# A hybrid attention and delta-rule block: frozen engine orders and four value blocks as seven half products

## The chip, the cores and the metric

The kernel runs on one core of a Trainium2 chip. The metric is the device time of one execution in microseconds, as a median of several. TensorE is called PE in the profile, VectorE DVE, ScalarE ACT, GpSimd POOL and SyncE SP.

## The reference

One residual layer on x of 1024 tokens by 1024 channels in float32. After an RMS norm, one input projection of 8208 columns feeds two mixers and their gates:

```python
h = _rmsnorm(x, norm_w[layer])
proj = h @ w_in[layer]
dsa_qkv, dsa_z, gdn_qkv, gdn_z, gdn_b, gdn_a, gate_a, gate_b = _split_columns(proj)
# mixer A: three groups of 8 heads x 64, windows and dilations (128,1), (512,4), (2048,16)
q_a = _apply_rope(qkv[:, :, :, 0], cos, sin)
k_a = _apply_rope(qkv[:, :, :, 1], cos, sin)
v_a = qkv[:, :, :, 2]
o_a = _dilated_mixture(q_a, k_a, v_a).astype(x.dtype)
y_a = (o_a * jax.nn.silu(dsa_z)) @ w_up_a[layer]
# mixer B: gated delta rule, 8 heads x 64, in chunks of 64 tokens, after a short causal conv
o_b = _gated_delta_rule(gq, gk, gv, g, beta)
y_b = (o_b * jax.nn.silu(gdn_z)) @ w_up_b[layer]
merged = jax.nn.sigmoid(gate_a) * y_a + jax.nn.sigmoid(gate_b) * y_b
x = x + merged @ w_out[layer]
```

A final RMS norm follows. The values v_a of the three groups are what the first half of the change touches: each is a plain product of h with 512 columns of w_in.

## The kernel before

**Numbers.** Each float32 operand of a projection is split into two float16 parts, hi and lo. A product is then three float16 matmuls per k tile (hi x hi, hi x lo, lo x hi), issued by `mm3_steps` (L183 to L185). The split is two instructions: ScalarE writes hi (`w_hi`, L166, or L330), VectorE writes lo with a `scalar_tensor_tensor` (the helper at L83, as a plain `tensor_tensor` is at L86).

**Units.** The input projection is cut in units of 256 output columns: 18 for attention (`att_unit(g, hs, what)`: group, half of the heads, and query, key or value), 6 for the delta rule, 4 of SiLU gates and 8 of sigmoid gates. A unit's weights come by two DMAs of 512 KB on GpSimd's queue into `wstage` (two buffers), and are split into `whi` and `wlo` (two buffers each). There are two kinds of unit. `Normal` multiplies all of h by the unit. `Seven` cuts h and the unit in halves both ways and forms seven products of half size in place of eight, from sums of the blocks of h (made once, `sums_of_h`) and of the weights (made per unit on VectorE, L329). `seven_products` runs them in three PSUM banks, with three ScalarE copies (L367) of a product that enters two outputs. The list `SEVENS` says which units are `Seven`: before, the queries and keys of groups 1 and 0, three sigmoid gates and all four SiLU gates.

Queries, keys and gates have channels on the output partitions, so the stationary operand is the weight block and 512 tokens stream past it (`proj`, `by_channel`). Values have tokens on the partitions: the stationary operand is 128 tokens of h, and the unit's 256 columns stream past it (`v_unit`, `gen`; matmuls `ps_mm<-whi,h_hi` of 128x256). Group 1 takes its 128 tokens at a stride of four (`tok`), group 2 at eight, group 0 packed.

**Order of TensorE.** TensorE's instructions are in the order of the program text, which interleaves two things by hand: `Feed` gives out the units in steps of some 0.65 us, and the attention (`att_run`), the delta rule's pieces and its scan take steps between them at set paces. `Feed.ahead` places the load and the splits of the next unit at set steps of the present one. In the attention's step, scores go to PSUM, VectorE masks them and takes the minimum (L799, tile `sm`), ScalarE takes the exponential (L803), TensorE transposes (L813), ScalarE and VectorE split the result into `th` and `tl` (L818, L86), and TensorE multiplies by the values (L836 to L840).

**Order of the others.** VectorE, ScalarE and the DMA queues are ordered by the framework's own scheduler, with hints: `tc.high_priority` around what evicts PSUM, `SOLVE_LATER` for the triangular solve, and `in_turn`, which ties some instructions to a place behind the matmul issued last in the text:

```python
def in_turn(i):
    if last_pe[0]:
        tc.add_manual_dep(i.ins, last_pe[0], order_only, reason="in turn")
```

Two stretches are fixed by hand on VectorE and ScalarE as well, with `manual_schedule`: the start (until the first query and key products are done) and the end of the last pair of token tiles.

**Stages, in us of the profile:** start to 62, attention beside the input units to 560, delta rule's preparation beside its units (convolutions `ca`, decay, solve, merge, `state_parts` with the copies `uw`) to 785, scan over 16 chunks beside the SiLU and gate units to 912, up projections to 995, output projection to the end.

Of the kernel before, what the change touches and what calls it, by code (L numbers as in the profile page):

```python
# [2 lines left out]

# [30 lines left out]
def att_unit(g, hs, what):  # L34
    return U_ATT + (g * 2 + hs) * 3 + what


def gdn_unit(hb, what):
# [39 lines left out]
def hybrid_block(ctx: ExitStack, tc: tile.TileContext, A):  # L78
# [7 lines left out]
        (eng or V).tensor_tensor(out, in0, in1, op)  # L86

    ctx.enter_context(tc.manual_schedule(engines={nc.tensor.engine}))
    base = ctx.enter_context(tc.tile_pool(name="base", bufs=1))
    ps = ctx.enter_context(tc.tile_pool(name="ps", bufs=1, space=PSUM))  # L90

# [57 lines left out]
    first = base.tile([128, 1], F32, name="first")  # L149
    SC.activation(first, epsc, AF.Sqrt)  # L150

    last_pe = [None]
    order_only = mybir.DependencyInfo(mybir.DependencyClass.NoSync, mybir.DependencyReason.DATA)

    def in_turn(i):

        if last_pe[0]:
            tc.add_manual_dep(i.ins, last_pe[0], order_only, reason="in turn")

    def load_w(src, c, n=256, eng=None):  # L160
        st = wst.tile([128, 4, n], F32, name="wstage", tag="wstage", bufs=2)
        (eng or nc.gpsimd).dma_start(out=st, in_=src[c])
        return st

    def w_hi(st, hi, c):
        in_turn(SC.activation(hi[:, 4 * c:4 * c + 4], st, AF.Copy, scale=W_SCALE))  # L166
# [10 lines left out]
    def mm3_steps(out, w, mov, ks=range(KT), first=True, last=True):  # L177

        wh, wl = w
        mh, ml = mov  # L180
        ks = list(ks)
        for i, k in enumerate(ks):
            PE.matmul(out, lhsT=wh(k), rhs=mh(k), start=first and i == 0, stop=False, skip_group_check=True)  # L183
            PE.matmul(out, lhsT=wh(k), rhs=ml(k), start=False, stop=False, skip_group_check=True)  # L184
            last_pe[0] = PE.matmul(out, lhsT=wl(k), rhs=mh(k), start=False, stop=last and i == len(ks) - 1,  # L185
                                   skip_group_check=True).ins.name
            yield

    def mm3(*a, **kw):
# [108 lines left out]
    class Seven:  # L298
# [18 lines left out]
        def split(self, n):  # L317
            if n < self.split_done:
                return
            self.load()  # L320
            self.split_done = n + 1
            t = w_tile(("whi", "wlo")[n % 2]).rearrange("p k c -> p (k c)").rearrange("p (b l n) -> p b l n", l=2, n=512)
            for b, name in enumerate(self.PAIRS[n]):
                if name not in self.part:

                    x, y = {"11+21": ("11", "21"), "11+21+22": ("11+21", "22"), "21+22": ("21", "22"),
                            "11+12+21+22": ("11+21+22", "12")}[name]
                    self.part[name] = self.part[x]
                    in_turn(V.tensor_tensor(self.part[name], self.part[x], self.part[y], ALU.add))  # L329
                in_turn(SC.activation(t[:, b, 0], self.part[name], AF.Copy, scale=W_SCALE))  # L330
# [162 lines left out]
        load_x(i)  # L493
    qk = [[bank("mm", 3), bank("mm", 3)], [bank("S", 2), bank("S", 2)]]
    ss = base.tile([128, 8], F32, name="ss0")
    with tc.manual_schedule(engines={nc.vector.engine, nc.scalar.engine}):
        wq, wk = w_first
        q, k = qk
        TT(nwd, ident[:, None, :].to_broadcast([128, KT, 128]), normw[:, :, None].to_broadcast([128, KT, 128]), ALU.mult)
        nwr = [bank("mm", 3), bank("O", 1)]  # L500
        for c in range(2):
            PE.matmul(nwr[c], lhsT=ones0, rhs=nwd[:, 4 * c:4 * c + 4].rearrange("p a b -> p (a b)"), start=True, stop=True)
# [60 lines left out]
        for ct in range(2):  # L563
            quarter(q[ct], wq, ct, 2)
# [393 lines left out]
    def sums_of_h(k):  # L958

        x = {}  # L960
        for i in range(2):
            room = rp.tile([128, 2, 512], F32, name="hx", tag="rt" if i == 0 else "rx", bufs=1 + i)
            for j in range(2):
                x[i, j] = room[:, j]
                ts = slice(512 * j, 512 * j + 512)
                in_turn(V.tensor_tensor(x[i, j], h_hi[:, 4 * i + k, ts], h_lo[:, 4 * i + k, ts], ALU.add))
# [553 lines left out]
    def load_sig(dt):  # L1520
        if dt < 4:
            sig["a", dt] = kp.tile([128, 16, 64], F32, name=f"sga{dt}", tag="kT", bufs=4).rearrange("p a b -> p (a b)")
        elif dt < 8:
            sig["a", dt] = late[2].tile([128, S], F32, name=f"sga{dt}", tag="sga", bufs=4)
        else:
            return
        sig["b", dt] = token_tile(f"sgb{dt}", "sgb")
        for br in "ab":
            in_turn(nc.sync.dma_start(out=sig[br, dt], in_=gsp[br, dt]))

    def load_wo(u):
        wos[u] = []
# [6 lines left out]
    def split_wo(kk):  # L1539
# [2 lines left out]

        def put(n, x):
            hi, lo = [y(kk) for y in wo7[n]]
            in_turn(SC.activation(hi, x, AF.Copy, scale=W_SCALE))
            STT(lo, x, W_SCALE, hi, ALU.mult, ALU.subtract)

        put(0, b11)
        in_turn(V.tensor_tensor(b11, b11, b12, ALU.subtract))
        put(4, b11)  # L1550
        TT(b12, b22, b12, ALU.subtract)
        put(1, b12)
# [9 lines left out]
    def m_parts(k, hf):  # L1562
# [7 lines left out]

        def put(n, y):
            hi, lo = [m7[hf][n][:, l, kk].rearrange("p (a i) -> p a i", a=2) for l in range(2)]
            in_turn(SC.activation(hi, y, AF.Copy, scale=M_SCALE))
            STT(lo, y, M_SCALE, hi, ALU.mult, ALU.subtract)

        if k < 4:
# [262 lines left out]
    for pair in range(4):  # L1839
# [50 lines left out]
        if pair == 3:  # L1890
# [16 lines left out]
                                       accum_out=out)  # L1907

            c1, c2 = [half(1, x) for x in parts]
            with tc.manual_schedule(engines={nc.vector.engine, nc.scalar.engine}):  # L1910
# [27 lines left out]
                V.tensor_scalar(o[:, 384:704], o[:, 384:704], r, None, op0=ALU.mult)  # L1938
                nc.sync.dma_start(out=A["out"][last.tk, 384:704], in_=o[:, 384:704])
                nc.scalar.dma_start(out=A["out"][last.tk, 704:], in_=o[:, 704:])  # L1940

# [103 lines left out]
```

## Time and profile before

| what | value |
|---|---|
| median of the runs | 1075.65 us |
| the profiled execution | 1076.42 us, span 1074.6 us |
| TensorE busy (its matmuls) | 1048.8 us, 98%, 9410 instructions |
| weight loads | 640.7 us, 60% |
| VectorE | 864.8 us, 80%, 1986 instructions |
| ScalarE | 560.9 us, 52%, 1274 instructions |
| GpSimd | 56.3 us, 5% |
| granted TensorE clock | 0.997 |
| DMA | 148.47 MB, mean 138 GB/s |

A busy time is the union of an engine's instructions, so overlapping matmuls count once; the end of a matmul is modelled. A wait row reads: engine, tile and line that waited, then who released it, total us, times, longest us. A group row reads: line, engine, operation, out<-in, shapes, count, then busy us, mean ns of one, and the idle time before them with what ended it.

### The profile page before, as it was taken

The numbers are of one execution on the slowest core, as the hardware profiler recorded it, in microseconds if no ns is written. First come the engines' busy times: TensorE is split into PE (matmuls) and PEld (weight loads), VectorE is DVE, ScalarE is ACT, GpSimd is POOL, SyncE is SP. The second block draws the span as 40 slices with busy tenths as digits, with TensorE's granted clock in tenths as the row PEclk, the third lists the DMA queues.
The fourth block names the chain that finished last, engine by engine and source line by source line (L and its number), as shares of the span: only waits on it lengthen the run. The fifth ranks groups of instructions, "written<-read, shape, count | busy, mean of one in ns | idle before, by whom it ended". The sixth has DMA issues, their size and how long they took to land.

```text
span 1074.6 us, 23700 instructions
## 1 busy us (share of the span) xinstructions
PE 1048.8 (98%) x9410; PEld 640.7 (60%) x9410; DVE 864.8 (80%) x1986; ACT 560.9 (52%) x1274; POOL 56.3 (5%) x107
## 2 busy tenths in 40 slices
PE   7999999999999999999999999999999999999997
PEld 5994685775956855765645545555555555444444
DVE  6997997869879779979966997986488679899844
ACT  6455766566666656547735733234344346343523
POOL 0000000000000000000000000110200000000000
PEclk9999999999999999999999999999999999999999
DMA  8144531632625432641234357786685433763132
GB/s 278 60 133 103 139 104 54 171 98 87 181 69 154 108 103 63 177 115 46 76 123 165 84 130 205 237 240 164 184 267 174 140 99 116 286 209 123 48 131 79
DMA packets 99776, 148.47 MB, mean 138 GB/s; under 512 B 31168, under 2 KB 64704, under 8 KB 98512
## 3 DMA queue, kind: packets, MB, share of 16 engines
q1 hardware_dynamic: 69264, 84.64, 27.3%
q0 software_dynamic: 12320, 44.11, 13.1%
q10 hardware_dynamic: 18080, 18.20, 4.9%
q8 instruction: 74, 1.21, 0.5%
q14 instruction: 38, 0.31, 0.1%
HBM read 91.13 MB, written 36.90 MB: 119 GB/s over the span
## 4 chain that ended last, share of the span: by engine, by line
PE 60%; DVE 27%; ACT 5%; issue 3%; DMA 3%; SPq 1%; ACTq 0%; DVEq 0%
PE ps_mm L183 14%; PE ps_mm L184 14%; PE ps_mm L185 14%; DVE ca L83 4%; DVE wlo L83 2%; DVE X L86 2%; DVE stmp L86 2%; DVE sm L799 2%; PE ps_S L185 2%; PE ps_S L184 2%; PE ps_S L183 2%; DVE tl L86 1%; PE ps_G L813 1%; DVE rt L86 1%; ACT sm L803 1%
## 5 line engine op out<-in xcount | busy, mean ns | idle before, releaser
L185 PE MATMUL ps_mm<-h_hi,wlo 128*128 128x512 f16 (+1 forms) x552 | 207.9, 377 | 0.0
L183 PE MATMUL ps_mm<-h_hi,whi 128*128 128x512 f16 (+1 forms) x492 | 185.5, 377 | 0.0
L184 PE MATMUL ps_mm<-h_lo,whi 128*128 128x512 f16 (+1 forms) x492 | 185.3, 377 | 0.0
L185 PEld LDWEIGHTS <-wlo 128*128 128x128 f16 x788 | 77.2, 98 | 86.5 <-issue 0.7
L183 PEld LDWEIGHTS <-whi 128*128 128x128 f16 x848 | 83.3, 98 | 69.1 <-issue 0.6
L184 PEld LDWEIGHTS <-whi 128*128 128x128 f16 x848 | 83.1, 98 | 67.9 <-issue 0.9
L183 PE MATMUL ps_mm<-whi,h_hi 128*128 128x256 f16 x384 | 105.1, 274 | 0.0
L185 PE MATMUL ps_mm<-whi,h_lo 128*128 128x256 f16 x384 | 104.7, 273 | 0.0
L184 PE MATMUL ps_mm<-wlo,h_hi 128*128 128x256 f16 x384 | 104.7, 273 | 0.0
L803 ACT ACTIVATE sm<-sm,osb 128x128 f32<-128x128 f32 (+1 forms) x160 | 69.5, 435 | 65.3 <-DVE osb L799 58.7
L86 DVE TENSOR_TENSOR tl<-ps_G,th 128x256 f16<-128x256 f32 (+1 forms) x96 | 51.8, 539 | 22.1 <-ACT th L818 21.6
L799 DVE CUSTOM_DVE_ANT_0 sm<-ps_S,amask 128x128 f32<-128x128 f32 (+1 forms) x192 | 59.2, 345 | 6.0 <-PE ps_S L792 5.9
L83 DVE SCALAR_TENSOR_TENSOR wlo<-wstage,whi 128x1024 f16<-128x1024 f32 x50 | 60.9, 1217 | 3.4 <-ACT whi L166 3.2
L83 DVE SCALAR_TENSOR_TENSOR ca<-xc,cw,ca 128x512 f32<-128x512 f32 x72 | 53.8, 747 | 5.5 <-ACT ca L1010 4.8
L166 ACT ACTIVATE whi<-wstage 128x1024 f16<-128x1024 f32 x49 | 51.4, 1051 | 1.7 <-ACT gst L948 0.8
L813 PE MATMUL ps_G<-cons,sm 128*128 128x128 f32 x280 | 47.9, 275 | 3.2 <-ACT sm L803 1.5
L83 DVE SCALAR_TENSOR_TENSOR whi<-wstage,whi 128x512 f16<-128x512 f32 x60 | 40.8, 687 | 12.3 <-ACT whi L330 11.7
L330 ACT ACTIVATE whi<-wstage 128x512 f16<-128x512 f32 x60 | 37.1, 626 | 19.6 <-DVE wstage L329 13.3
L813 PEld LDWEIGHTS ps_G<-cons,sm 128*128 128x128 f32 x280 | 35.5, 141 | 19.4 <-ACT sm L803 5.0
L184 PEld LDWEIGHTS <-h_hi 128*128 128x128 f16 x384 | 45.8, 119 | 1.6
L183 PE MATMUL ps_mm<-h_hi,wlo 128*128 128x512 f16 x120 | 45.6, 380 | 1.0 <-DVE rx L83 1.0
L183 PEld LDWEIGHTS <-h_hi 128*128 128x128 f16 x384 | 45.5, 119 | 1.5
(459 smaller groups left out, 2595.7 us busy)
## 6 DMA issues: line engine op xcount, KB each, us to landing
wstage<-in_w POOLq DMA_DIRECT2D x68, 512.0 KB, 4.5
og<-osb ACTq DMA_DIRECT2D x32, 132.0 KB, 2.2
og<-og SPq DMA_DIRECT2D x32, 132.0 KB, 2.2
gspb<-gst ACTq DMA_DIRECT2D x16, 256.0 KB, 2.4
sga<-gspa SPq DMA_DIRECT2D x8, 512.0 KB, 6.5
wstage<-in_w_up POOLq DMA_DIRECT2D x8, 512.0 KB, 4.7
wos<-in_w_out SPq DMA_DIRECT2D x8, 512.0 KB, 5.3
sgb<-gspb SPq DMA_DIRECT2D x8, 512.0 KB, 4.9
```

The costliest lines, as they stand in the source:

```text
L83: (eng or V).scalar_tensor_tensor(out, in0, scalar, in1, op0=op0, op1=op1)
L86: (eng or V).tensor_tensor(out, in0, in1, op)
L166: in_turn(SC.activation(hi[:, 4 * c:4 * c + 4], st, AF.Copy, scale=W_SCALE))
L183: PE.matmul(out, lhsT=wh(k), rhs=mh(k), start=first and i == 0, stop=False, skip_group_check=True)
L184: PE.matmul(out, lhsT=wh(k), rhs=ml(k), start=False, stop=False, skip_group_check=True)
L185: last_pe[0] = PE.matmul(out, lhsT=wl(k), rhs=mh(k), start=False, stop=last and i == len(ks) - 1, skip_group_check=True).ins.name
L330: in_turn(SC.activation(t[:, b, 0], self.part[name], AF.Copy, scale=W_SCALE))
L799: V.tensor_tensor_reduce(P[:, u, :128 * nk], psc[:, u * 256:u * 256 + 128 * nk], mask, -cexp, -NEG, ALU.add, ALU.min, accum_out=osb[:, 256 ...
L803: SC.activation(P[:, u, :128 * nk], P[:, u, :128 * nk], AF.Exp, bias=osb[:, 256 + hd:257 + hd], scale=-1.0, accum_out=osb[:, 260 + hd:261 ...
L813: PE.transpose(pt[:, c:c + 128], P[:, u, i * 128:i * 128 + 128], ident)
```

## The change

`SEVENS` takes in the four value units of groups 1 and 0. Their generator `gen7` with `by_token`, which stood in the kernel without use, forms each of the seven half products as four pieces of 128 tokens by 128 columns, on 4 k tiles each: 28 steps for 32. Two of the four outputs are the difference of a product and a kept one, for which VectorE takes one more instruction and a rotation buffer (`rope_room`).

All of `in_turn` goes; the two stretches fixed by hand become `in_order()`, which only records where they lie. At the end of the program `set_orders` goes over all instructions: it finds their dependencies and the reuse of buffers, gives each a cost from its shape, and runs a model of the engines three times forward with two backward runs between. A backward run gives each instruction its latest start; a forward run lets each engine take, of the instructions whose inputs are there, the one with the earliest latest start. TensorE keeps the order of the text. The best forward run's order is written down for VectorE, ScalarE, GpSimd and SyncE, each instruction behind the one before it on its engine. The cost model holds prices such as `150 + 1.0417 * n` ns for VectorE with n elements per partition, and for a DMA a time to landing.

```diff
-SEVENS = ([att_unit(g, hs, w) for g in (1, 0) for hs in range(2) for w in range(2)]
+SEVENS = ([att_unit(g, hs, w) for g in (1, 0) for hs in range(2) for w in range(3)]
           + [U_GATE + i for i in (0, 6, 7)] + [U_Z + i for i in range(4)])
...
     def w_hi(st, hi, c):
-        in_turn(SC.activation(hi[:, 4 * c:4 * c + 4], st, AF.Copy, scale=W_SCALE))
+        SC.activation(hi[:, 4 * c:4 * c + 4], st, AF.Copy, scale=W_SCALE)
...
-    with tc.manual_schedule(engines={nc.vector.engine, nc.scalar.engine}):
+    with in_order():
...
+    set_orders(tc, fixed)
...
+        elif self.kind == "InstDMACopy":
+            kb = w[0].total / 1024
+            self.hold, self.ns, self.pass_ns = 330 + 0.25 * kb, 2000 + (2.2 if w[0].dram else 5.5) * kb, 60
+            if min(w[0].piece, r[0].piece) < 256:
+                self.hold = 1400 if kb > 64 else 600
+                self.ns = self.hold + 2500
+            if self.eng == "POOL":
+                self.hold = 530
+        elif self.eng == "DVE":
+            one = len(r) == 1
+            self.ns = {"InstMemset": 60 + 0.5 * n, "InstReciprocal": 150 + 6.2 * n, "InstTensorCopy": 160 + 0.55 * n}.get(
+                self.kind, 150 + 1.0417 * n)
+            if self.kind == "InstTensorScalarPtr":
+                self.ns = 150 + 0.53 * n if one else self.ns + 60 * (len(r) > 2)
+            self.hold = self.ns - 83
...
+def fill(steps, rank, back):
...
+            while due[e] and due[e][0][0] <= t:
+                i = heapq.heappop(due[e])[1]
+                heapq.heappush(open_[e], (rank[i], i))
...
+            i = heapq.heappop(open_[e])[1]
+        s, extra = steps[i], 0
+        if not back and s.table not in (0, table):
+            table, extra = s.table, TABLE_NS
...
+        start[i], free[e] = t, t + s.hold + extra
+        order[e].append(i)
...
+def set_orders(tc, in_order):
+
+    steps = steps_of(tc, in_order)
+    rank = [float(s.i) for s in steps]
+    best = None
+    for _ in range(PASSES):
+        start, order, end = fill(steps, rank, False)
+        if best is None or end < best[0]:
+            best = end, order
+        late = fill(steps, [-t for t in start], True)[0]
+        rank = [-t - s.hold for s, t in zip(steps, late)]
+    start, order, end = fill(steps, rank, False)
+    if end < best[0]:
+        best = end, order
+    order_only = mybir.DependencyInfo(mybir.DependencyClass.NoSync, mybir.DependencyReason.DATA)
+    for e, ids in best[1].items():
+        if e != "PE":
+            for a, b in zip(ids, ids[1:]):
+                tc.add_manual_dep(steps[b].ins, steps[a].ins.name, order_only, reason="engine order")
```

More of the change, by code (lines that the diff above doesn't have):

```diff
@@ L1 @@
-from contextlib import ExitStack
+import heapq
+from contextlib import ExitStack, contextmanager
 from itertools import zip_longest
@@ L184, in mm3_steps @@
             PE.matmul(out, lhsT=wh(k), rhs=ml(k), start=False, stop=False, skip_group_check=True)
-            last_pe[0] = PE.matmul(out, lhsT=wl(k), rhs=mh(k), start=False, stop=last and i == len(ks) - 1,
-                                   skip_group_check=True).ins.name
+            PE.matmul(out, lhsT=wl(k), rhs=mh(k), start=False, stop=last and i == len(ks) - 1, skip_group_check=True)
             yield
@@ L1909, in hybrid_block @@
             c1, c2 = [half(1, x) for x in parts]
-            with tc.manual_schedule(engines={nc.vector.engine, nc.scalar.engine}):
+            with in_order():
                 mean(eo[:, 2:3], eo[:, 0:1], epsc)
@@ L1940, in hybrid_block, with __init__, mask, meets @@
                 nc.scalar.dma_start(out=A["out"][last.tk, 704:], in_=o[:, 704:])
+    set_orders(tc, fixed)
+ENGINES = {"PE": "PE", "DVE": "DVE", "Activation": "ACT", "Pool": "POOL", "SP": "SP"}
+TABLES = {"Exp": 1, "Tanh": 1, "Sqrt": 2, "Silu": 3, "Ln": 4}
+SIZES = {F32: 4, F16: 2, BF16: 2}
+SBUF_BYTES = 212832
+TABLE_NS = 1283
+TILE_SWITCH_NS = 150
+PASSES = 2
+class Operand:
+    def __init__(self, b, write):
+        size = SIZES[b.dtype]
+        ap = [tuple(x) for x in b.ap]
+        self.name, self.size, self.write, self.dram = b.tensor.name, size, write, "DRam" in type(b.tensor).__name__
+        self.psum = b.tensor.name.startswith("ps_")
+        if self.dram:
+            self.rows, first, free = (0, 1), b.offset * size, ap
+        else:
+            row = int(np.prod(b.tensor.shape[1:])) * SIZES[b.tensor.dtype] // size
+            p = b.offset // row
+            self.rows, first, free = (p, p + (ap[0][1] if ap[0][0] else 1)), b.offset % row * size, ap[1:]
+        self.free = free
+        self.cols = int(np.prod([n for _, n in free]))
+        self.bytes = (first, first + size + sum(abs(s) * (n - 1) * size for s, n in free))
+        self.total = self.cols * size * (1 if self.dram else ap[0][1])
+        self.piece = size
+        for s, n in reversed(free):
+            if s * size != self.piece and n > 1:
+                break
+            self.piece *= n
+    masks = {}
+    def mask(self):
+        key = self.bytes[0], self.size, tuple(self.free)
+        if key not in self.masks:
+            at = np.zeros(1, dtype=np.int64)
+            for s, n in self.free:
+                if s:
+                    at = (at[:, None] + (s * np.arange(n))[None, :]).ravel()
+            bits = np.zeros((int(at.max()) + 1, self.size // 2), dtype=np.uint8)
+            bits[at] = 1
+            self.masks[key] = int.from_bytes(np.packbits(bits, bitorder="little").tobytes(), "little") << (key[0] // 2)
+        return self.masks[key]
+    def meets(self, o):
+        if not self.psum and not all(a[0] < b[1] and b[0] < a[1] for a, b in ((self.rows, o.rows), (self.bytes, o.bytes))):
+            return False
+        return self.dram or self.psum or (self.mask() & o.mask()) != 0
@@ new lines, in steps_of, with behind @@
+def steps_of(tc, in_order):
+    steps = [Step(i, ins) for i, ins in enumerate(tc.nc.cur_bb.bb.instructions)]
+    written, read, users, place = {}, {}, {}, {}
+    for s in steps:
+        for x in s.args:
+            for j, y in written.get(x.name, []) + (read.get(x.name, []) if x.write else []):
+                if j not in s.deps and x.meets(y):
+                    s.deps.add(j)
+        for x in s.args:
+            (written if x.write else read).setdefault(x.name, []).append((s.i, x))
+            users.setdefault(x.name, set()).add(s.i)
+        s.deps.discard(s.i)
+    def behind(later, earlier):
+        for i in later:
+            steps[i].deps.update(j for j in earlier if j < i)
+    for t in tc.info.tiles:
+        if t.name in users:
+            place.setdefault((t.owner_uid, t.tag or t.name), []).append(t)
+    for ts in place.values():
+        ts.sort(key=lambda t: min(users[t.name]))
+        slots = [None] * ts[0].tag_meta.bufs
+        for a, b in zip([None] + ts, ts):
+            n = min(range(len(slots)), key=lambda n: max(users[slots[n].name]) if slots[n] else -1)
+            for i in users[b.name]:
+                steps[i].turn |= {min(users[a.name])} if a else set()
+                steps[i].deps |= users[slots[n].name] if slots[n] else set()
+            slots[n] = b
+    areas, open_, shut = {}, {"left": 0, "right": 0}, {}
+    pools = {p.name: p for p in tc.info.pools if p.space == bass.MemoryType.SB}
+    used = {f"_{n}_{p.id}": set() for n, p in pools.items()}
+    for t in tc.info.tiles:
+        for n in used:
+            if (t.tag or "").endswith(n):
+                used[n] |= users.get(t.name, set())
+    for s in steps:
+        if s.kind != "BassTilePoolBoundary" or s.ins.bass_pool_name not in pools:
+            continue
+        p = pools[s.ins.bass_pool_name]
+        side = str(p.side).split(".")[-1].lower()
+        total = sum(m.bufs * -(-m.max_size_bytes // 128 // m.align_bytes) * m.align_bytes for m in p.tag_meta.values())
+        if s.ins.op != "alloc":
+            open_[side] -= total
+            shut[p.name] = areas[p.name]
+            continue
+        lo = open_[side] if side == "left" else SBUF_BYTES - open_[side] - total
+        open_[side] += total
+        areas[p.name] = lo, lo + total
+        for n, (a, b) in shut.items():
+            if lo < b and a < lo + total:
+                behind(used[f"_{p.name}_{p.id}"], used[f"_{n}_{pools[n].id}"])
+    for a, b in in_order:
+        last = {}
+        for s in steps[a:b]:
+            if s.eng in ("DVE", "ACT") and s.kind != "InstDMACopy":
+                if s.eng in last:
+                    s.deps.add(last[s.eng])
+                last[s.eng] = s.i
+    for s in steps:
+        s.deps = {j for j in s.deps if steps[j].eng}
+        s.turn -= s.deps | {s.i}
+        for j in s.deps | s.turn:
+            steps[j].succ.append(s.i)
+    return steps
```

119 lines of the change are left out of this document (107 added, 12 removed).

## The prediction

> **What bounds the kernel now.** I read the busy times first, then TensorE's waits, then busy time by stretch, and last the durations of the operations that the change adds.
>
> ```profile
> span 1074.6 us, 23700 instructions
> PE 1048.8 (98%) x9410; PEld 640.7 (60%) x9410; DVE 864.8 (80%) x1986; ACT 560.9 (52%) x1274; POOL 56.3 (5%) x107
> ```
>
> TensorE is busy 98% of the span: the kernel is bound by the list of matmuls, and another engine's work costs something only where a matmul waits for it. The profiled execution took 1076.42 us, 1.8 us outside its span; it lies 0.8 us above the median of 1075.65. I make the sum against 1076.42 and subtract 0.8 at the end. About 2%, 21.5 us, is what a measurement of this kernel can tell from no change.
>
> ```profile
> PE ps_mm L502 <- DVE nwd L86: 5.3, 1, 5.3
> PE ps_O L840 <- DVE tl L86: 2.7, 3, 1.3
> PE ps_S L1266 <- ACT uw L1424: 2.3, 1, 2.3
> PE ps_G L813 <- ACT sm L803: 1.5, 4, 0.6
> PE ps_G L813 <- DVE tl L86: 1.2, 1, 1.2
> PE ps_mm L183 <- DVE rx L83: 1.0, 1, 1.0
> PE ps_mm L478 <- DVE h_lo L83: 1.0, 1, 1.0
> PE ps_mm L478 <- DVE wlo L83: 0.8, 2, 0.5
> PE ps_O L836 <- ACT osbs L845: 0.5, 1, 0.5
> PE ps_S L1755 <- DVE zb L83: 0.5, 1, 0.5
> PE ps_O L1247 <- DVE rq L1251: 0.4, 1, 0.4
> PE ps_G L1365 <- DVE Y L86: 0.4, 1, 0.4
> ```
>
> Columns: who waited for whom, total us, times, longest. Of these rows L502 and L478 lie in the start, whose VectorE and ScalarE order is fixed before and after. The other nine sum to 10.5 us (four more, of 0.2 to 0.3 us, lie below). A busy matmul is counted past the point where the next could start, so the true loss is larger: 14 waits times some 0.16 us (a 128x512 matmul lasts 379 ns at a spacing of 216) is an estimate of 2.3 us more. With a half-clock spell after 760 us (below) the waits that an order could remove come to about 14 us. That is all a better order has to win.
>
> ```profile
> 62.00:160.00 98.00, 96.44 (x774) 71.25 (x772) 85.55 (x180) 58.62 (x141) 3.18 (x6) 1.00 0.48 126
> 160.00:297.50 137.50, 137.50 (x1162) 98.77 (x1161) 111.91 (x263) 88.33 (x242) 6.35 (x12) 1.00 0.42 119
> 297.50:410.00 112.50, 112.50 (x889) 72.43 (x887) 89.47 (x237) 71.78 (x193) 5.30 (x10) 1.00 0.35 101
> 410.00:547.50 137.50, 131.60 (x1185) 87.14 (x1184) 127.51 (x407) 84.72 (x223) 5.82 (x11) 1.00 0.35 100
> 700.00:785.00 85.00, 81.92 (x1104) 44.10 (x1096) 54.49 (x98) 35.03 (x63) 12.94 (x23) 0.98 0.69 201
> 410.00:460.00 50.00, 48.93 (x421) 35.08 (x420) 49.23 (x131) 30.16 (x75) 3.18 (x6) 1.00 0.50 137
> 760.00:765.00 5.00, 2.70 (x69) 1.78 (x67) 0.19 (x1) 1.45 (x3) 1.39 (x3) 0.88 0.95 221
> 765.00:770.00 5.00, 5.00 (x78) 2.46 (x77) 3.17 (x6) 0.63 (x1) 0.56 (x1) 0.78 0.41 149
> ```
>
> Columns: stretch, length, busy PE, weight loads, DVE, ACT, POOL, granted clock, DMA share, GB/s. The losses sit in three places: 1.6 us in 62–160, 5.9 in 410–547.5, 3.1 in 700–785 with, behind it, a clock of 0.88 and 0.78 for two slices of 5 us (an estimate: 0.12 and 0.22 of 5 us, of which about 1.2 us fell on matmuls). In 410–460 VectorE is busy 49.23 of 50 us. There it is the second bound, and that is where the new value blocks add to it.
>
> **The change: the value products.** A value block is now 8 token tiles x 8 k x 3 = 192 matmuls of 256 columns; as seven half products it is 7 x 4 x 4 x 3 = 336 of 128 columns.
>
> ```profile
> 40.23 0.27 PE L183 MATMUL ps_mm<-h_hi,whi 128*128 128x256 f16 x1
> 42.74 0.27 PE L185 MATMUL ps_mm<-h_hi,wlo 128*128 128x256 f16 x1
> 19.80 4.02 PE ps_mm L478 x72
> ```
>
> The first two rows are the first and last of 24 matmuls of 256 columns: 2.51 us over 23 steps, 109.1 ns each. The third, from the chain, is 72 matmuls of 128 columns, each with a weight load of its own: 55.8 ns each. So 192 x 109.1 = 20.95 us becomes 336 x 55.8 = 18.75 us, 2.2 us saved per block and 8.8 us for four. An eighth fewer columns doesn't give the full eighth, since short matmuls pay their fixed part more often.
>
> ```profile
> L183 PEld LDWEIGHTS <-h_hi 128*128 128x128 f16 x64 | 7.3, 114 | 0.1
> L183 PEld LDWEIGHTS <-h_hi 128*128 128x128 f16 x64 | 6.3, 98 | 0.7
> L1076 PEld LDWEIGHTS <-h_lo 128*128 128x128 f16 x64 | 3.2, 96 | 0.0
> ```
>
> Groups of weight loads in 200–225, 342–369 and 467–471.5 us. Group 1 reads its weights at a stride of four tokens (first row: 114 ns) where group 0 reads them packed (98). In the third row packed loads feed 16-column matmuls 25 ns apart, so a load occupies far less than it lasts; 25 + 16 = 41 ns for the strided one is still under 55.8. Bounds: nothing, or all 16 ns exposed, 336 x 71.8 = 24.1 us, which would turn the saving of the two group 1 blocks into a loss of 3.2 us each. I take nothing, the value nearest to the third row.
>
> The Trainium skill ("TensorE: Matmul & The Clock Gate", Back-to-back issue gap) speaks against this part: it gives a stream of load and matmul pairs some 81 ns at 128 columns. By that figure, an estimate from that page, a block would take 27.2 us, 6.3 us more than now. The row of 72 such pairs at 55.8 ns disagrees, and the measurement decides.
>
> **What the value blocks put on the other engines.**
>
> ```profile
> L83 DVE SCALAR_TENSOR_TENSOR wlo<-wstage,whi 128x1024 f16<-128x1024 f32 x50 | 60.9, 1217 | 3.4 <-ACT whi L166 3.2
> L83 DVE SCALAR_TENSOR_TENSOR whi<-wstage,whi 128x512 f16<-128x512 f32 x60 | 40.8, 687 | 12.3 <-ACT whi L330 11.7
> L329 DVE TENSOR_TENSOR wstage<-wstage 128x512 f32<-128x512 f32 x60 | 40.7, 685 | 0.4
> L166 ACT ACTIVATE whi<-wstage 128x1024 f16<-128x1024 f32 x49 | 51.4, 1051 | 1.7 <-ACT gst L948 0.8
> L330 ACT ACTIVATE whi<-wstage 128x512 f16<-128x512 f32 x60 | 37.1, 626 | 19.6 <-DVE wstage L329 13.3
> L367 ACT COPY ps_mm<-ps_mm 128x512 f32<-128x512 f32 x30 | 17.2, 574 | 23.1 <-PE ps_mm L185 22.6 <-ACT osb L845 0.4
> L83 DVE SCALAR_TENSOR_TENSOR gst<-ps_mm,x 128x512 f32<-128x512 f32 x6 | 4.1, 686 | 0.1
> ```
>
> VectorE per block: seven splits (7 x 0.687) and four sums (4 x 0.685) for two splits (2 x 1.217), and two subtractions of the kept product at eviction (2 x 0.686): 4.81 + 2.74 - 2.43 + 1.37 = 6.5 us, 26 us for four. ScalarE: 7 x 0.626 + 3 x 0.574 - 2 x 1.051 = 4.0 us, 16 for four, beside 561 of 1075: hidden, with over 45% of its time left. The two 512 KB loads on POOL's queue keep their size; the staging buffer comes free later, after the last sum. The subtracted product takes one of two rotation buffers for a moment, and behind it ScalarE's next rotation copy would wait, which holds a PSUM bank. Both I cost at nothing, covered by the neighbouring query and key blocks, which already run as sevens in this stage with single waits of 1 us; if that cover went, it would be such a 1 us wait per block, 4 us.
>
> VectorE decides. In 160–297.5 (the two group 1 blocks) it needs 111.9 + 13 = 124.9 us against 137.5 - 4.4 = 133.1 of TensorE: 94%. That still fits: the 4.4 us come through, less perhaps 0.5. In 297.5–547.5 (group 0) it needs 89.5 + 127.5 + 13 = 230.0 us. TensorE without any wait needs 250 - 8.5 (the 5.9 and its share of the refill) - 4.4 = 237. So VectorE must be busy 97% for 237 us on end to give it all. If it reaches only the 92.7% of 410–547.5, the stretch takes 248 us, 2 us less than now; at the 98.4% of 410–460 it would take TensorE's 237, 13 less. I take 95%, between the two rows: 242 us, 8 less.
>
> **The order.** Counts of instructions don't change by it. The old hints (priorities, the delay of the solve, the "in turn" ties to a matmul) give way to four frozen lists: VectorE, ScalarE, POOL's and SP's queues, each instruction behind the one before it, by latest start in a model of the kernel. Moved queries, keys and weights take their DMAs along, past others on SP's and POOL's queues. The first 38 us and the last 15 keep their VectorE and ScalarE order, so the 5.3 us wait for `nwd` and the tail stay. Outside the attention stage I see 1.6 us in 62–160 and about 4.5 around 760 to win. The latter is ScalarE's copy `uw` waiting for the landing of an earlier copy, with three buffers for four copies; the model charges landings too little (next part). I take 3 of 6 us. Bounds: 6 gained, or as much lost again by new waits.
>
> Sum: 1076.4 - (4.4 - 0.5) - 8 - 3 = 1061.5; less 0.8, about **1061 us**, 1.4% faster.
>
> **Rivals.**
> 1. *All waits go.* VectorE holds 97% and the other stretches lose nothing: 4.4 + 13 + 6 = 23.4, so 1052 us. For it: 98% over 50 us is on record. Against: there it had a queue of ready work because it was itself late.
> 2. *VectorE becomes the bound.* The freed matmul time turns into waits for the weight splits and evictions: 2 us from group 0, 4 from group 1, 0 to 3 elsewhere: 1067 to 1070; with new waits outside, up to 1077. For it: the 92.7% above. That the order does no better than the old one lands here too (8.8 us of matmuls: 1067).
> 3. *The frozen lists stop on late data, slower.* Each VectorE instruction waits at the head of its list for its input; if that comes later than in the model, everything behind it waits, and TensorE with it.
>
> ```profile
> T1p<-t_d SPq DMA_DIRECT2D x4, 128.0 KB, 8.2
> MT<-u_d SPq DMA_DIRECT2D x8, 128.0 KB, 6.1
> wn_d<-uw ACTq DMA_DIRECT2D x8, 256.0 KB, 3.3
> ```
>
>  These are landings (last number, us). The model has 2.6 us for the last (2000 + 2.2 x 256 ns) and 3.9 for the other two (1400 + 2500 ns, its price for short pieces). From 160 to 547.5 VectorE's 328.9 us become 355. That stretch takes 355/u at a busy share u: at 0.916 nothing is won, and from 0.868 (409 us, 21.5 more than 387.5) the kernel is slower by 2%. At 0.85, which is the share it has there now, it is 418 us, 30 more: 1106. Against: the other prices in the model lie close to the rows (687 ns measured, 683 modelled for a 128x512 split), and the late landings belong to the delta-rule stage, where VectorE has room. The Trainium skill ("TensorE: Matmul & The Clock Gate", Architectural detail) calls VectorE and ScalarE strict FIFOs; no row here shows what lies behind a waiting instruction.
> 4. *Weight loads pace the short matmuls.* At the loads' own 98 and 114 ns, blocks take 32.9 and 38.3 us: 2 x 12.0 + 2 x 17.4 = 59 us more than now, 1128 with some 7 us won by the order. The 55.8 ns speak against it.
>
> **Chances.** My forecast (1054 to 1067) 0.53; all waits go 0.17; VectorE the bound (1067 to 1077) 0.20; frozen lists 0.08; weight loads 0.02. Faster by over 2% means under 1054.1: 0.17. Slower by over 2%: 0.10. Within 2%: 0.73. The range takes in the forecast, most of the first rival and the second: 1049 to 1077.
>
> **What would show it.** Matmuls of 128 columns at L183 to L185, 1344 of them, 56 ns apart, the group 1 ones too; DVE busy near 890 us; DVE at 94 to 96% between 300 and 540 us; TensorE's idle under 6 us after the start, with the waits for `tl` and `sm` shorter but not gone; the 760 us wait halved, perhaps without the half clock. Wrong would make it: strided loads that pace (71 ns), a VectorE share well below 92% with PE waiting for `whi`, `wlo` or `tl`, or new waits for a landing after 600 us.

## The result and the profile after

The changed kernel takes 1086.03 us (median of four runs, 1085.18 to 1087.47) against 1075.1 for the kernel before: a ratio of 1.0105, 95% interval 1.0085 to 1.0125. One of the four runs of the kernel before took 2809.53 us; it counts in that median and not in the ratio. The change is 1% slower, where 1061 was forecast and 1077 was the upper end of the range. The profiled execution took 1086.27 us with a span of 1084.5, 9.9 us more than before.

Span and busy times of the page of after:

```profile
span 1084.5 us, 24950 instructions
PE 1047.0 (97%) x9986; PEld 639.9 (59%) x9986; DVE 879.6 (81%) x2030; ACT 572.0 (53%) x1306; POOL 56.1 (5%) x107
```

576 more matmuls and 44 more VectorE instructions are there, as the value blocks demand, and VectorE is busy 14.8 us more. TensorE's busy time has hardly fallen, though its list is shorter; the clock explains that below. The waits of TensorE in after (who waited for whom, total us, times, longest):

```profile
PE ps_mm L502 <- DVE nwd L87: 5.2, 1, 5.2
PE ps_G L813 <- ACT sm L803: 4.5, 3, 3.5
PE ps_S L1266 <- ACT uw L1424: 3.9, 1, 3.9
PE ps_mm L184 <- DVE Vl L84: 3.5, 1, 3.5
PE ps_O L840 <- DVE tl L87: 1.8, 4, 0.6
PE ps_mm L478 <- DVE h_lo L84: 1.7, 2, 1.0
PE ps_S L790 <- issue: 1.6, 1, 1.6
PE ps_O L1247 <- DVE rq L1251: 1.4, 1, 1.4
```

Many small waits became few large ones. The `tl` waits of before (2.7 and 1.2 us) are 1.8; but three stops of 3.5 to 3.9 us stand there, where the largest after the start was 2.3. Over all rows of the two views, after has some 11 us more of waits than before (29.5 against 18.7). Each large stop also costs something behind it. Busy time by stretch in after (stretch, length, busy PE, weight loads, DVE, ACT, POOL, granted clock, DMA share, GB/s):

```profile
200.00:312.00 112.00, 105.22 (x1222) 78.22 (x1221) 92.85 (x216) 73.22 (x196) 5.27 (x10) 0.98 0.45 125
410.00:555.00 145.00, 140.73 (x1389) 93.44 (x1387) 136.67 (x442) 92.98 (x240) 6.33 (x12) 0.98 0.37 104
305.00:310.00 5.00, 5.00 (x24) 2.65 (x23) 1.01 (x7) 3.01 (x11) 0.48 (x1) 0.72 0.30 108
485.00:490.00 5.00, 3.91 (x12) 1.91 (x13) 4.89 (x22) 4.50 (x16) 0.00 (x0) 0.53 0.08 23
490.00:495.00 5.00, 5.00 (x28) 2.62 (x27) 4.13 (x14) 1.89 (x7) 0.00 (x0) 0.79 0.09 26
770.00:775.00 5.00, 5.00 (x70) 2.80 (x69) 1.29 (x2) 0.00 (x0) 0.56 (x1) 0.50 0.28 94
```

Behind each stop the granted clock is 0.50 to 0.79. The four 5 us slices lose 5 x (0.28 + 0.47 + 0.21 + 0.50) = 7.3 us of full clock, where before lost 1.7 around 760 us; TensorE looks busy there because its matmuls are slower. Less the idle time in the second slice, that is an estimate of 5 us more. So: 8.8 us off the list, 11 us of new idle time and 5 us of half clock on it, 7 of the 9.9 us in all. The remaining 3 us are not assigned. TensorE's busy time fits this: its busy time times the missing part of the clock, over all 5 us slices after the start, comes to 7.4 us in after and 1.4 before. Without that it would have fallen by 7.8 us, near the 8.8 of the list (an estimate).

**How a stop comes about** is seen at 298 us. First SyncE's queue in after (start, us, operation), then VectorE, then TensorE:

```profile
296.51 0.59 SPq L629 DMA_DIRECT2D Ks<-pch  x1
297.15 1.22 SPq L629 DMA_DIRECT2D Ks<-pcl  x2
298.41 1.55 SPq L870 DMA_DIRECT2D og<-og  x3
```

```profile
297.55 0.68 DVE L84 SCALAR_TENSOR_TENSOR Vl<-rx,Vh 128x512 f16<-128x512 f32 x1
303.29 0.17 DVE L873 COPY md<-og 128x16 f32<-128x16 f32 x1 [5.06 <-DMA og<-og]
303.38 0.68 DVE L84 SCALAR_TENSOR_TENSOR Vl<-ps_mm,Vh 128x512 f16<-128x512 f32 x1
```

```profile
304.11 0.38 PE L184 MATMUL ps_mm<-sum1h,whi 128*128 128x512 f16 x1 [3.53 <-DVE Vl L84]
```

A 64 KB copy of keys takes SyncE 0.59 us to issue, one every 0.63 us; the model has 330 + 0.25 x 64 = 346 ns. With sixteen such copies ahead that makes a difference of some 4.5 us: by the model the `og` loads of the mixture would be out that much earlier. (The model's own times are on no record; this is worked out from its price.) The first `og` load goes out at 298.41 and VectorE can read it at 303.29, 4.9 us later, which is itself about twice the usual landing (more on that below). `md<-og` is at the head of VectorE's list, so VectorE idles 5.06 us although the eviction `Vl<-ps_mm` behind it is ready, and TensorE waits for the PSUM bank of just that eviction. The stop at 482 us is alike, on ScalarE, again behind sixteen copies of keys (462.43 to 473.70 us on SyncE's queue); its rows in after, and TensorE's:

```profile
477.42 0.28 ACT L1080 ACTIVATE ba<-ps_O 128x128 f32<-128x128 f32 x1 [4.40 <-DMA og<-og]
...
485.54 0.40 ACT L803 ACTIVATE sm<-sm,osbs 128x128 f32<-128x128 f32 x1
```

```profile
486.09 0.86 PE L813 MATMUL ps_G<-cons,sm 128*128 128x128 f32 x2 [3.47 <-ACT sm L803]
```

`ba` waits 4.40 us for a landing, and the exponential that TensorE needs stands behind it in the list, 8 us later. In those 8 us ScalarE's list has mainly the small steps for the decay, with two more waits for VectorE (1.58 and 1.35 us) and two loads of an activation table (1.28 us each). At 765 us it is the `uw` wait of before, longer.

### The profile page after: what moved, and what is told of

Read it like the earlier page. It is cut to its first block, busy times and chain, and to the rows that moved or that the text cites. A ratio compares the mean times of both kernels' runs of the same rounds, so it can differ in the third digit from the quotient of the medians.

```text
span 1084.5 us, 24950 instructions
## 1 busy us (share of the span) xinstructions
PE 1047.0 (97%) x9986; PEld 639.9 (59%) x9986; DVE 879.6 (81%) x2030; ACT 572.0 (53%) x1306; POOL 56.1 (5%) x107
## 3 DMA queue, kind: packets, MB, share of 16 engines
q8 instruction: 78, 1.28, 0.5%
## 4 chain that ended last, share of the span: by engine, by line
PE 41%; DVE 14%; issue 3%; DMA 3%; ACT 3%; POOL 0%; ACTq 0%; DVEq 0%; SPq 0%; POOLq 0%
PE ps_mm L184 10%; PE ps_mm L186 9%; PE ps_mm L185 9%; DVE ca L84 3%; PE ps_S L186 1%; PE ps_S L185 1%; PE ps_S L184 1%; DVE sm L799 1%; DVE tl L87 1%; DVE wlo L84 1%; PE ps_G L186 1%; PE ps_G L185 1%; PE ps_G L184 1%; DMA wn_d<-uw 1%; PE ps_S L1706 1%
## 5 line engine op out<-in xcount | busy, mean ns | idle before, releaser
L84 DVE SCALAR_TENSOR_TENSOR wlo<-wstage,whi 128x1024 f16<-128x1024 f32 x42 | 51.1, 1220 | 17.5 <-ACT whi L167 15.7
L330 ACT ACTIVATE whi<-wstage 128x512 f16<-128x512 f32 x76 | 46.0, 626 | 32.0 <-DVE wstage L329 9.8
L185 PE MATMUL ps_mm<-wlo,h_hi 128*128 128x256 f16 (+1 forms) x256 | 57.3, 246 | 0.0
L84 DVE SCALAR_TENSOR_TENSOR whi<-wstage,whi 128x512 f16<-128x512 f32 x76 | 51.9, 686 | 6.6 <-ACT whi L330 6.2
L167 ACT ACTIVATE whi<-wstage 128x1024 f16<-128x1024 f32 x41 | 42.7, 1053 | 22.0 <-PE ps_mm L185 11.6
L329 DVE TENSOR_TENSOR wstage<-wstage 128x512 f32<-128x512 f32 x76 | 52.1, 688 | 1.1
L818 ACT CAST th<-ps_G 128x256 f16<-128x256 f32 (+1 forms) x96 | 43.8, 456 | 5.3 <-PE ps_G L813 4.4
L184 PE MATMUL ps_mm<-whi,h_hi 128*128 128x256 f16 (+1 forms) x192 | 46.5, 256 | 0.0
L186 PE MATMUL ps_mm<-whi,h_lo 128*128 128x256 f16 (+1 forms) x192 | 46.2, 255 | 0.0
```

The lines of the kernel that those rows point to most:

```text
L84: (eng or V).scalar_tensor_tensor(out, in0, scalar, in1, op0=op0, op1=op1)
L818: SC.copy(th[:, :n], pt[:, :n])
```

## The experiments

In every run the kernel before ran on the same chip: 1074.5 to 1075.6 us.

**The two halves by themselves.** Both edit `SEVENS`, the first from the kernel after as below, the second from the one before, the other way round:

```diff
-SEVENS = ([att_unit(g, hs, w) for g in (1, 0) for hs in range(2) for w in range(3)]
+SEVENS = ([att_unit(g, hs, w) for g in (1, 0) for hs in range(2) for w in range(2)]
```

> The new order with the old units (values of groups 1 and 0 as 192 matmuls of 256 columns). Late-data theory: the order itself loses, so this is as slow as the changed kernel or slower by the 8.8 us of matmuls that it does not save: 1084 to 1094 us, with VectorE still stopped for over 3 us at a copy that waits for a landing. VectorE-load theory: without the 26 us that the value blocks add to VectorE the order works: 1064 to 1073 us.

> The old order with the four value blocks as sevens. Late-data theory: the value blocks are innocent, TensorE's list is 8.8 us shorter and VectorE takes the extra work at the price of a few short waits: 1066 to 1073 us. VectorE-load theory: VectorE cannot take the 26 us in the attention stage, and waits for weight splits and evictions eat the gain and more: 1078 to 1092 us.

Measured: the order alone 1098.65 us, 1.022 [1.0195, 1.0246]; the value blocks alone 1084.38, 1.0099 [1.0067, 1.013]. Each half alone is slower: by 23 and by 9 us, and the first lies above both ranges that were expected for it. They don't add: under the new order the value blocks take 12.6 us off (1098.65 to 1086.03), under the old one they add 9. Each of these kernels has its own frozen lists, so part of the 12.6 can be the lists' luck (more on that below). VectorE's and ScalarE's waits for landings with the order alone:

```profile
DVE md L873 <- DMA og<-og: 13.8, 4, 6.4
DVE xc L1005 <- DMA Ks<-pcl: 6.7, 1, 6.7
```

```profile
ACT ea L1094 <- DMA Ks<-pcl: 8.1, 1, 8.1
```

Before, `md` waited 4.7 us in three times, 1.9 at most. The stretch from 410 to 472 us, of before and then with the value blocks alone, and in the latter TensorE's largest wait after the start:

```profile
410.00:472.00 62.00, 59.58 (x625) 44.17 (x624) 56.57 (x155) 32.21 (x81) 3.18 (x6) 1.00 0.50 135
```

```profile
410.00:472.00 62.00, 53.88 (x607) 39.66 (x606) 60.75 (x157) 37.13 (x92) 3.17 (x6) 0.97 0.44 115
```

```profile
PE ps_G L899 <- DVE osb L86: 5.5, 1, 5.5
```

VectorE is busy 60.75 of 62 us, 4.2 more, and TensorE 53.88, 5.7 less: here VectorE is the bound. So each half loses time by itself, and in another way.

**One price in the model** (from the kernel after; for the second run, also 1.5 us on every landing):

```diff
             if self.eng == "POOL":
                 self.hold = 530
+            if self.eng == "SP" and not (w[0].dram or r[0].dram):
+                self.hold = 630
...
+            self.ns += 1500
```

> The changed kernel with one price of its model raised: SyncE's issue of a copy within the chip's memory, 0.35 us in the model, 0.63 us in the profile of the changed kernel. Nothing else differs but the order that follows. Late-data theory: the loads of og come off SyncE in time, the 5.06 us stop of VectorE at md near 298 us goes, with the half clock behind it: 1076 to 1083 us. VectorE-load theory: 1083 to 1089 us, VectorE as busy and TensorE waiting elsewhere.

> As the run before, and every DMA's time to landing raised by 1.5 us in the model. Late-data theory: the model now sets VectorE's and ScalarE's instructions that wait for a landing behind work that is ready, so most of the stops go: 1060 to 1076 us. VectorE-load theory: 1083 to 1090 us.

Measured: 1077.47 us, 1.0022 [1.0001, 1.0043], and 1077.54, 1.002 [1.0007, 1.0032]. With the measured issue price the kernel takes 8.6 us less; a longer landing on top wins nothing and falls between the two ranges. With the price alone, the same place (the trace is of the fastest of its ten runs, 1073.17 us):

```profile
293.10 2.50 SPq L629 DMA_DIRECT2D Ks<-pcl  x4
295.64 1.61 SPq L870 DMA_DIRECT2D og<-og  x3
```

The `og` loads go out 2.8 us earlier, `md` waits 2.29 us here and 3.0 in all, and the 3.5 us stop for `Vl` is gone.

**Group 1's value blocks alone, in the old order** (from before; VectorE has room in that stage):

```diff
-SEVENS = ([att_unit(g, hs, w) for g in (1, 0) for hs in range(2) for w in range(2)]
+SEVENS = ([att_unit(g, hs, w) for g in (1, 0) for hs in range(2) for w in range(2 + (g == 1))]
```

> The old order with only the two value blocks of group 1 as sevens, where VectorE had 19% of its time free. If VectorE's load decides, they give their 4.4 us: 1070 to 1073 us, and the loss of the run with four blocks (8.8 us) came from group 0's two. If sevens of values cost the old order something in any place: 1076 to 1082 us.

Measured: 1079.84 us, 1.0042 [1.0028, 1.0055]: 4.4 us slower, 8.8 us above what two shorter blocks should give. The stretch that holds most of the blocks, before and in that kernel (its trace is of the fastest of five runs, 1077.39 us):

```profile
200.00:300.00 100.00, 100.00 (x900) 78.04 (x898) 81.61 (x185) 63.36 (x167) 3.25 (x7) 1.00 0.46 126
200.00:300.00 100.00, 96.94 (x1178) 73.80 (x1177) 89.31 (x198) 67.54 (x177) 4.22 (x8) 1.00 0.46 124
```

VectorE needs only 89%, and TensorE still loses 3.1 us, in waits for `sm` (1.1), `tl` (1.0) and `Vl` (0.7) that are not there before. So VectorE's share is not all of it. Whether the old hints place the added work badly, or the form of the seven products costs something (its banks, kept copies and borrowed buffer), no run tells, and the rest of the 8.8 us has no place in this trace.

**A price that should not matter** (from after: the time a result takes to reach the next engine):

```diff
-        self.table, self.small, self.hold, self.ns, self.pass_ns = 0, False, 0, 0, 35
+        self.table, self.small, self.hold, self.ns, self.pass_ns = 0, False, 0, 0, 45
```

> The changed kernel with a harmless price of its model altered, the time from a VectorE or ScalarE result to another engine, 45 ns for 35. This shuffles the lists without mending SyncE's price. Late-data theory: the stop of VectorE at md behind SyncE's rotation copies stays in kind, 1082 to 1092 us. Chance theory (any other order would have gained what the right issue price gained): it may land anywhere, 1074 to 1090 us, and a time at or below 1079 speaks for it.

Measured: 1088.57 us, 1.0128 [1.0106, 1.0151], 2.5 us slower than after. This one other order, without a better price, doesn't give the 8.6 us of the issue price. But in it, too, the stop at `md` shrinks (to 2.15 us) and the `Vl` row goes, while other stops come. So these two signs don't prove the price's part, and one draw doesn't rule out luck in the 8.6.

**The other two stops mended** (from the issue price). SyncE's loads of the start are held in the order of the text, and the fourth `uw` copy gets a buffer of its own:

```diff
+    last = None
+    for s in steps[:in_order[0][1]]:
+        if s.eng == "SP" and s.kind == "InstDMACopy":
+            if last is not None:
+                s.deps.add(last)
+            last = s.i
...
-                    uw = p2_.tile([128, 4, 2, 64], F32, name="uw", tag="rv", bufs=3)
+                    if x and r:
+                        uw = wst.tile([128, 512], F32, name="uw4", tag="x7", bufs=1)
...
```

> The run with SyncE's issue price, and two stops taken away: SyncE's loads of the start keep the order of the text (2.2 us of TensorE's waits came in there), and every fourth copy uw before the scan gets a buffer of its own (two waits of 2 to 4 us near 760, with the half clock). Late-data theory: 1069 to 1074 us. If freed waits only move on: 1076 to 1079 us.

Measured: 1070.25 us, 0.9956 [0.9941, 0.9971]. That is 7.2 us less than with the price alone. TensorE's largest rows after the start's are then:

```profile
PE ps_G L813 <- ACT sm L803: 3.8, 4, 2.5
PE ps_O L840 <- DVE tl L87: 1.9, 3, 0.7
PE ps_O L1247 <- DVE rq L1251: 1.3, 1, 1.3
PE ps_mm L184 <- ACT gst L948: 1.2, 1, 1.2
```

The `uw` row is down to 0.7 us.

**One value block less** (from the issue price, the last value unit of group 0 in its old form):

```diff
-SEVENS = ([att_unit(g, hs, w) for g in (1, 0) for hs in range(2) for w in range(3)]
+SEVENS = ([att_unit(g, hs, w) for g in (1, 0) for hs in range(2) for w in range(3 - (g == 0 and hs == 1))]
```

> The run with SyncE's issue price, but the last value block (group 0, second half of the heads, where VectorE is full) in the old form. If VectorE's load decides there, the 2.2 us of matmuls that come back are more than repaid: 1070 to 1076 us. If the new order already fits it in: 1078 to 1082 us.

Measured: 1088.58 us, 1.0122 [1.0101, 1.0144], 11 us more than with that block as a seven and above both expected ranges. As a seven it saves 2.2 us of matmuls, so 9 us come from elsewhere. TensorE's waits of this kernel:

```profile
PE ps_mm L184 <- ACT gst L948: 4.0, 1, 4.0
PE ps_S L1266 <- ACT uw L1424: 3.6, 1, 3.6
PE ps_O L840 <- DVE tl L87: 3.0, 5, 1.0
```

A stop of 4.0 us at `gst`, ScalarE's copy of a gate on its way to DRAM, where after has 1.0, and one at `uw`, both with the issue price right. All its rows sum to 29.4 us, where the issue price's kernel has 21.0: with the 2.2 us of matmuls that is nearly the whole difference. So the price is not the only cause: where the stops fall changes with the program, here by about 10 us.

**The value blocks in the mended order, and a longer landing** (from the mended kernel of the experiment before the last; `range(2)` in `SEVENS`, and `self.ns += 1500`):

> The best run so far (right issue price, start in the order of the text, a fourth buffer) with all four value blocks in the old form: what they are worth under the mended order. If VectorE's load costs them nothing there, the 8.8 us of matmuls come back: 1077 to 1081 us. If the load eats their gain, as in the old order: 1066 to 1073 us.

> The best run with every landing 1.5 us later in the model. Late-data theory: the remaining stops behind landings (ScalarE at gst near 391 us, at the delta rule's first small products near 474) shrink: 1064 to 1069 us. If the margin only moves urgency about: 1069 to 1078 us.

Measured: without the value blocks 1082.09 us, 1.0062 [1.0045, 1.008], so they are worth 12 us in the mended order, and that order without them is still 7.6 us slower than before; with the longer landing 1071.51, 0.9974 [0.9963, 0.9985], no gain. The kernel without the value blocks has these waits for landings on VectorE, and on TensorE these stops:

```profile
DVE md L873 <- DMA og<-og: 6.2, 3, 5.7
DVE xc L1005 <- DMA og<-og: 5.5, 1, 5.5
```

```profile
PE ps_G L813 <- ACT sm L803: 4.7, 2, 4.1
PE ps_mm L184 <- ACT gst L948: 4.5, 1, 4.5
```

The lists stop again at the mended price, in two ways. The `og` loads at `md` are not slow to land here: VectorE reaches `md` at 292.14 us, SyncE issues the first load at 295.47, and it is read at 297.86. Why SyncE is that late in this order is not shown. The stop at `gst` is a slow landing: the gate's way to DRAM (256 KB) takes 5.6 us from 391.79, where it took 2.8 in after.

**What a slow landing goes with** can be read from these traces. The three `og` loads near 298 us have a median landing of 4.1 to 4.5 us in the six kernels in which GpSimd issues a 512 KB weight load within 0.7 us of the first of them (after is one, at 297.93), and of 2.1 to 2.6 us in the ten in which it doesn't. The slow landing at `gst` has such a load 0.5 us behind its issue. This is seen side by side, not tested by a change; the model has one price for both.

**The fourth buffer in the old order** (the buffer's edit alone, on before):

> The kernel before with the fourth buffer for uw alone: how much of the best run's gain needs no new order. The 2.3 us wait near 760 with its half clock (1.2 us) goes: 1071 to 1074 us if it is a true loss; 1075 to 1077 if another wait takes its place.

Measured: 1071.83 us, 0.9971 [0.9961, 0.9982]. That is 0.3%, some 3 us, for the wait at 760 us and the half clock behind it, with neither half of the change.

**VectorE's load by itself, in the old order.** Two tries at adding 24 us of VectorE work to the value blocks and nothing else. The first repeats the weights' `wlo` split (`again` is 3 and 2 for the two parts of these units, 0 elsewhere); the second repeats a `scalar_tensor_tensor` in place behind an eviction, where nobody waits for it soon. Both leave all values as they were:

```diff
-            w_lo(self.st[c], *self.blocks, c)
+            for _ in range(1 + self.again[c]):
+                w_lo(self.st[c], *self.blocks, c)
```

```diff
                                 STT(vl, p, H_SCALE * P_SCALE, vh, ALU.mult, ALU.subtract)
+                                if g < 2 and jj < 3:
+                                    for _ in range(3):
+                                        STT(vl, vl, 1.0, vl, ALU.mult, ALU.max)
```

> The kernel before, values as 192 matmuls, but VectorE writes each lo half of the four value blocks' weights several times over (20 more splits of 1.217 us, 24 us, the same numbers): the load of the sevens without their matmuls. VectorE-load theory: as much lost as the run with old order and four sevens lost against its shorter list, some 17 us: 1086 to 1098 us. If the sevens lose by their form (banks, copies, the borrowed buffer): 1075 to 1081 us.

> The kernel before with 36 more VectorE operations of 128x512 in the four value blocks (24.7 us), each rewriting a finished low half of values with itself, well ahead of its use: VectorE's load without late weights. VectorE-load theory: the old order loses much of it in VectorE's full stretch, 1083 to 1095 us. If load alone is absorbed and only late weights cost: 1075 to 1080 us.

Measured: 1097.84 us, 1.0213 [1.0198, 1.0229], and 1083.43, 1.0074 [1.0057, 1.0091]. The first says little: in it TensorE waits for the repeats themselves, which stand ahead of the weights' first use:

```profile
PE ps_mm L184 <- DVE wlo L83: 15.5, 6, 4.7
```

The second shows more of the load:

```profile
410.00:472.00 62.00, 55.81 (x483) 39.54 (x481) 60.33 (x152) 33.33 (x82) 3.16 (x6) 0.99 0.47 124
```

```profile
PE ps_G L902 <- DVE osb L86: 5.8, 1, 5.8
```

It is the 5.5 us wait of the value blocks alone, at the same place with the same VectorE share: 24.7 us of VectorE work cost 8.1 us of time. The value blocks alone lost 17.6 us against their shorter list, so load of this kind is less than half of it. For the rest there are their later weights, of which the first try shows that they can cost, and their form; no run parts these.

**The gates' spill off SyncE** (from the mended kernel, without and with the longer landing):

```diff
-        eng = nc.scalar if (br, dt // 2) > ("a", 0) else nc.sync
-        eng.dma_start(out=gsp[br, dt][:, hf * 512:hf * 512 + 512], in_=t)
+        nc.scalar.dma_start(out=gsp[br, dt][:, hf * 512:hf * 512 + 512], in_=t)
```

> The best run with the four spills of gate 0's first channels on ScalarE's queue, as all other spills are, in place of SyncE's. Before, ScalarE's next tanh into the one buffer gst waited for such a spill, and TensorE behind it, near 391 us. Late-data theory: that stop (1.2 us) goes: 1067 to 1070 us. If it makes no odds where the spill is issued: 1070 to 1073 us.

> The run with later landings in the model, and the spills off SyncE's queue. There the stop at gst was 4.7 us, with a half clock of 3.4 us behind it. Late-data theory: 6 us less than that run, 1064 to 1067 us. Otherwise 1070 to 1073 us.

Measured: **1068.78 us**, 0.994 [0.9925, 0.9955], the lowest of all, and 1070.8, 0.9963 [0.9951, 0.9975]. The stop at `gst` was to go, and it stays: 1.1 us, where the mended kernel has 1.2, and with the longer landing 3.6 for 4.7. So the 1.5 us by which the first is faster than the mended kernel are not shown to come from the spill, and the intervals overlap. The best kernel beats before by 6.5 us. The fourth buffer alone gave some 3 of that, so the whole new order with the value blocks adds 3 to 4 us to it (a difference of two runs).

## Why the prediction was wrong

**TensorE's list: right.** The matmuls of 128 columns are 56 ns apart, the strided ones of group 1 too; twelve rows of a group 1 block in after, of which the first and the last (start, us, operation):

```profile
207.30 0.22 PE L184 MATMUL ps_mm<-wlo,sum2h 128*128 128x128 f16 x1
...
207.91 0.22 PE L186 MATMUL ps_mm<-wlo,sum2l 128*128 128x128 f16 x1
```

0.61 us over eleven steps is 55 ns. The weight loads' own durations (rival 4) do not pace them; the 8.8 us were there to be had. The Trainium skill ("TensorE: Matmul & The Clock Gate", Back-to-back issue gap) gives such a pair some 81 ns at 128 columns; this trace does not agree.

**VectorE's load: half right.** Busy times with the value blocks alone:

```profile
PE 1045.7 (97%) x9986; PEld 639.6 (59%) x9986; DVE 885.4 (82%) x2030; ACT 574.8 (53%) x1306; POOL 56.1 (5%) x107
```

"26 us" by single durations came out as 20.6 us of busy time in the old order (885.4 against 864.8) and as 20.9 in the new one (879.6 against 858.7 with the order alone). The step "I take 95%, between the two rows: 242 us, 8 less" failed in the form of its argument. A share needed over 250 us says nothing of the peaks: with the value blocks alone VectorE was full from 410 to 472 us, which cost TensorE 5.7 us there, while other stretches had room. Load put aside cost 8.1 us, about the matmuls' gain; that is rival 2, with its price of "4 from group 1" too low in the old order (8.8 by the run with group 1's blocks alone). But in the new order the blocks took off 12.6 us, where the prediction had 11.9 for them (4.4 - 0.5 and 8). That agreement is luck: the list accounts for 8.8 of it at most, and the rest came from stops that fell otherwise (wait rows of 29.5 us, where the order alone has 33.6).

**The order: the step that failed.** "I take 3 of 6 us", with a bound of as much lost again, stood where the order alone lost 23 us. In place of 3 us won, the term is 23 us lost, and it alone turns the sum. The prediction had the mechanism as rival 3, at a chance of 0.08, and dismissed it with "the late landings belong to the delta-rule stage, where VectorE has room". The stops came in the attention stage too, and a price that was not looked up has a part in them: SyncE's issue time. The rows of SyncE's queue were there to be read (0.59 us for each copy of a key or query), and the model's 0.346 was in the diff. The kernel with that price is 8.6 us faster, though how much of this is the price and how much another draw of the lists is not settled; with the price, the start and the fourth buffer mended, the order alone still lost 7.6 us. The share u at which the rival "decides" was the wrong scale too: after is slower with VectorE busy 94% from 410 to 555 us. What decides is which instruction the list stops on, and not how full the engine is.

**The half clock was counted only as something to win.** The prediction priced the spell after 760 us, but no new ones. Each new stop brought one, an estimate of 5 us.

**The start was left out of the sum: some 2 us.** VectorE's and ScalarE's order there is fixed, and the wait for `nwd` stayed as forecast. But SyncE's order is not fixed: its loads were moved, and `h_lo`, `h_hi` and `xt` came later (`h_lo` 1.7 us for 1.0). Mended together with `uw`, it gave 7.2 us.

Of the signs named in advance, the spacing of 56 ns came, and the 94% from 410 us on; VectorE's busy time, forecast near 890 us, was 879.6; "TensorE's idle under 6 us after the start" was some 20, the waits for `tl` became shorter (3.9 to 1.8 us), but those for `sm` grew from 1.5 to 4.5, and the `uw` wait was not halved but went from 2.3 to 3.9. The waits for a landing came long before 600 us.

**Still open.** Why the order without one value block is 11 us worse at the right issue price. Its stops are at `gst` and `uw` again. A longer landing in the model, the same for all, did nothing in three tries. The traces show slow landings beside a weight load; a model that has this was not tried. And what in the value blocks costs more than their load in the old order stays open.

## What to carry to other kernels

A frozen order is no better than the prices in the model behind it: before trusting it, lay each price beside its row, the issue times of the DMA queues first, because a list stops on one late item with ready work behind it. One right price did not make it safe here, so measure several variants before trusting one. Price a stop of TensorE with the half clock that follows it, and weigh added work on a second engine by its fullest 50 us, not by its mean; room there is needed, but was not enough for group 1's blocks. Where two parts of a change are measured, measure them together and apart: here +23 and +9 made +11.

## What the runs showed of the hardware

- Issuing a 64 KB copy from buffer to buffer occupies SyncE for 0.59 us, one every 0.63 us.
- An `og` load of 132 KB lands in 2.3 us at the median in after, and took 4.9 us from its issue to its reader at 298 us. Its row among the DMA issues (count, size, median us to landing):

```profile
og<-og SPq DMA_DIRECT2D x32, 132.0 KB, 2.3
```

- Three `og` loads together land in 4.1 to 4.5 us at the median with a 512 KB weight load issued within 0.7 us of them (six kernels), and in 2.1 to 2.6 without (ten kernels).
- The three longest stops of TensorE after the start, 3.5 to 3.9 us, were followed by a low granted clock: 0.72 in one 5 us slice, 0.53 then 0.79, and 0.50. Behind the stop at 482 us the matmuls of 512 columns start 0.43 us apart, where it is 0.22 otherwise. The Trainium skill ("TensorE: Matmul & The Clock Gate", Part 1: The HAM clock gate) puts the change to half rate behind an idle window of some 3.4 us; the traces agree on the half rate, but the 2.3 us stop of before had a spell too (0.88, then 0.78), with sparse work around it, and a 2.5 us wait for `rq` near 770 us in the best kernel had none.
- 44 more VectorE instructions, 26 us by their durations, made 20.6 to 20.9 us of busy time: two splits of 0.68 us in a row take 1.28 us.
